# A two-layer decoder trunk on one core: every sum of squares over folded halves, the rotation's sine step as one operation, and a new order

## Chip, core and metric

The kernel runs on one core of one Trainium2 chip. The metric is the device time of one execution in microseconds. The core has five engines with instruction queues of their own: TensorE (PE, matmuls; its weight loads are shown apart as PEld), VectorE (DVE), ScalarE (ACT), GpSimd (POOL) and SyncE (SP, which here only starts transfers). Each works through its queue in order, and they wait for one another through semaphores.

## The reference

Two layers over 512 positions of width 1024, all in float32. What bears on the change:

```python
def rmsnorm(x, g):
    xf = x.astype(jnp.float32)
    y = xf * lax.rsqrt(jnp.mean(xf * xf, axis=-1, keepdims=True) + EPS)
    return y.astype(x.dtype) * g

def rope(x, cos, sin):
    half = x.shape[-1] // 2
    x1, x2 = x[..., :half], x[..., half:]
    ...
    return jnp.concatenate([x1 * cos - x2 * sin, x2 * cos + x1 * sin], axis=-1)

def hybrid_layer(...):
    h = rmsnorm(x, norm_g)
    aq, ak, av, az, bqk, bv, bi, bf, bo, bz, ga, gb = jnp.split(h @ w_in, idx, axis=-1)
    q = rope(rmsnorm(two_map_heads(aq), q_norm_g), cos, sin)   # 8 heads, 2 maps of 64
    k = rope(rmsnorm(two_map_heads(ak), k_norm_g), cos, sin)
    oa = diff_attention(q, k, v, lam)                          # 8 heads of 128
    oa = rmsnorm(oa, attn_norm_g) * (1.0 - lam_init)
    ya = (oa * jax.nn.silu(az)) @ w_out_a
    ...
    hb = mlstm_chunkwise(mq, mk, mv, i_pre, f_pre)             # 8 heads of 128
    hb = rmsnorm(hb, mlstm_norm_g)
    yb = (jax.nn.sigmoid(bo) * hb * jax.nn.silu(bz)) @ w_out_b
    u = jax.nn.sigmoid(ga) * ya + jax.nn.sigmoid(gb) * yb
    return x + u @ w_o
```

## The kernel before, in words

**Products.** Every float32 operand of a matmul is split into a high part in a rounded float32 format and a low part, the rest: a copy on ScalarE (`A.copy(hi, src)`, a CAST in the profile) and a subtraction on VectorE (`split`, line 489). A product is then three matmuls: high by high, high by low, low by high (`mm3`, line 493). Weights come in blocks of 128x1024 (`wr`), and are split into `wh` and `wl`. The normalised input stands transposed as `hh` and `hl`. Projections into 512 tokens by 512 columns or 128 features by 512 tokens accumulate in PSUM tiles of 128x512, of which four (`acc`) are in turn. The last projection, `wo`, is done with seven products instead of eight (`seven`, line 763): P1 to P7 are added up in three PSUM chains, X, Y and Z. P5 and then P3 go into the two banks of Y. Between them ScalarE copies what P5 has left there into an SBUF tile, `p5` (line 779), which P7 needs. What P1 leaves in the two banks of X is copied into `s1` in the same way.

**Attention.** For each of eight heads and four query blocks: scores (`sc`), a mask, a maximum, the exponentials (`p`), the difference of the two maps, transpositions (`ut`) into the split tiles `uh` and `ul`, and then the product with the values (`av`, 12 matmuls and splits of 128 to 512 columns). For the output of a head, 128 features by 512 tokens, the mean of squares over the features is a sum over partitions. It is made by matmuls with a 128x128 matrix of ones (`psum_over`, line 1267), whose result, `msp`, has the sum in every partition. The mLSTM heads end alike (`num` in place of `av`); their denominator `den` is such a sum too.

**Two ways to make the sum.** `ms_front` (line 1271) squares the head's output. Unfolded, the square of 128x512 is split (`msh`, `msl`), and two matmuls with ones add it up. Folded, the two halves of the partitions are squared by two operations of 64x512 (`ms`, `fb`), VectorE adds the one to the other, the sum is split into the two halves of one tile (`fo`: partitions 0 to 63 the high part, 64 to 127 the low one), and one matmul with ones adds both up. `foldA` and `foldM` name the heads that are folded, in attention and in mLSTM; `foldD` the denominators, all of them folded already.

**Rotation.** `qk_done` (line 827) takes a block of 512 columns of q and k. VectorE multiplies it with the cosine table into `rot`, and its halves, exchanged, with the sine table into `sq`: one operation for the first halves of all heads, one for the second. The two are then added.

**The order.** Nothing is issued where the code stands. All operations are recorded first (`Recorder`, line 103): the pieces of the projections follow the list `order`, the heads' steps are hung in between at places given by `a0`, `ap`, `attn`, `m0`, `mp`, `ml` and others. Then `schedule` (line 272) sorts them anew: it gives each operation a due time by its place, its successors and the table `bias`, and takes for each engine in turn the ready operation that is due first, by its own costs and margins (`pemargin`, `smargin`, `late` and others). Each engine's queue is issued in this order. Every number in `TUNE` can so move instructions on all engines.

Of the kernel before, what the change touches and what calls it, by code (L numbers as in the profile page):

```python
# [13 lines left out]
ALU = mybir.AluOpType  # L14
# [4 lines left out]
P = 128  # L19
# [16 lines left out]

TUNE = {
    "order": (
# [4 lines left out]
    ),  # L43
    "qkt": 5,
    "gct": 15,
    "gls": 6,
    "glf": 5,
    "attn": (1, 5, 5, 8, 9, 13, 15, 16, 19, 24),
    "a0": 23,
    "ap": 18,  # L50
    "a4": 7,
    "ml": (1, 9, 11, 12, 13, 28),
    "ahead": 3,
    "lc": 7,
    "slack": 4956.0,
    "margin": 72.0,
    "pemargin": 171.8,
    "wait": 333.1,
    "swpen": 701284048.1,
    "smargin": 51.6,  # L60
    "pwait": 0.8,
    "wdiff": 3673.3,
    "wsp": 4,
    "kact": (0, 2),
    "qsq": (1, 3),
    "foldA": (2, 3, 5),
    "foldM": (0, 1, 2, 3, 4, 7),
    "foldD": (0, 1, 2, 3, 4, 5, 6, 7),
    "warm": 18,
    "start": 'x0 ct ng w0 x1 w1 x2 x3',  # L70
    "prods": 'P1 P5 P3 P6 P2 P7 P4',
    "acl": 12,
    "gateA": 9,
    "gateM": 0,
    "actp": (0, 2, 3),
    "m0": 218,
    "mp": 15,
    "m4": 11,
# [366 lines left out]
def kernel(ctx, tc, x, pos, wp, wg, cst, par, pb, ngb, out):  # L445
# [30 lines left out]
    V, A, T = rec.engine("DVE", nc.vector), rec.engine("ACT", nc.scalar), rec.engine("PE", nc.tensor)  # L476
# [3 lines left out]
    def t2(name, dt=F32):  # L480
        return s2.tile([P, S], dt, tag="s2", name=name)
# [19 lines left out]
    ct = cp.tile([P, C_N], F32, name="ct")  # L501
    posi = cp.tile([P, NT], I32, name="posi")
# [10 lines left out]
    ones = cp.tile([P, P], F32R, name="ones")  # L513
# [21 lines left out]
    cosv = cp.tile([P, NT, 32], F32, name="cosv")  # L535
    sinv = cp.tile([P, NT, 32], F32, name="sinv")
# [86 lines left out]
    x1d = dram.tile([S, D], F32, name="x1d")  # L623


    def layer_events(l):
# [200 lines left out]
        def qk_done(c, tt, acc):  # L827
# [584 lines left out]
        for c in range(4):  # L1412
            ps["qk%d" % c] = tok("qk", c, h_tok, qk_done)
# [227 lines left out]
```

## Time and profile before

| | |
|---|---|
| median of 3 runs | 1334.36 us (1334.33 to 1334.86) |
| profiled execution | 1334.56 us |
| its span | 1332.5 us |
| instructions | 17532 |
| TensorE clock granted | 1.00 |
| transfers | 148.14 MB, mean 111 GB/s |

The profile is one execution. A row of instructions reads: line, engine, operation, output<-inputs by the program's names, partitions by elements, count, and then busy time and mean duration, or (in a tile's view) the least, median and largest duration in ns with the first and the last start in us. A row of the timeline reads: start, duration, engine, line, operation, and in brackets the idle time before it with what ended it. Since all operations are issued by one helper, nearly all have line 441. The names say more: `msp_a` is the sum of squares of an attention head, `msp_b` that of an mLSTM head, `wo_P` the seven products. A matmul's duration reaches into those of its neighbours, so the distance from one start to the next is what it takes of the queue.

### The profile page before, as it was taken

To read this page: it belongs to the slowest core of one execution; us is meant where nothing else is said; L and a number is where in the kernel's file an instruction comes from. 1 tells how busy PE (TensorE), PEld (TensorE's weight loads), DVE (VectorE), ACT (ScalarE), POOL (GpSimd) and SP (SyncE) were. 2 spreads that over 40 slices of the span, in tenths; PEclk is the share of its full clock that TensorE was granted. 3 is DMA by queue.
4 is the path that set the end of the run, shared out by engine and by line. 5 is a ranking of instruction groups with operands and counts; after the bars stand their busy time and mean duration, and the time that the engine had idled before them with its cause. 6 is when DMAs were issued, how large, how long until landed. Compare 5 with 4: busy or idle time off the path is not lost.

```text
span 1332.5 us, 17532 instructions
## 1 busy us (share of the span) xinstructions
PE 1325.0 (99%) x6200; PEld 1095.0 (82%) x6200; DVE 1018.0 (76%) x1846; ACT 907.8 (68%) x1836; POOL 36.9 (3%) x44
## 2 busy tenths in 40 slices
PE   9999999999999999999999999999999999999998
PEld 7888888888888888888788888888888888888886
DVE  7898899786259968755888988997852699687566
ACT  6878798877247858743667787889762489687343
POOL 1000000000000000000200000000000000000000
PEclk9999999999999999999999999999999999999999
DMA  5222222223333443554833122222332344354646
GB/s 188 87 67 78 80 83 64 91 79 99 95 103 112 149 123 113 146 155 128 248 112 95 49 95 64 79 76 83 82 112 79 128 119 141 99 135 135 170 122 182
DMA packets 51272, 148.14 MB, mean 111 GB/s; under 512 B 6096, under 2 KB 12880, under 8 KB 51184
## 3 DMA queue, kind: packets, MB, share of 16 engines
q1 hardware_dynamic: 48880, 138.63, 32.9%
q0 software_dynamic: 2304, 8.39, 3.6%
q8 instruction: 49, 0.80, 0.2%
q14 instruction: 39, 0.32, 0.1%
HBM read 142.74 MB, written 4.26 MB: 110 GB/s over the span
## 4 chain that ended last, share of the span: by engine, by line
PE 98%; ACT 1%; DMA 0%; SPq 0%; DVE 0%; issue 0%; DVEq 0%
PE qk L441 13%; PE av L441 9%; PE az L441 7%; PE bv L441 7%; PE bqk L441 7%; PE bz L441 7%; PE bo L441 7%; PE gb L441 7%; PE ga L441 7%; PE woa L441 7%; PE wob L441 7%; PE wo_P L441 6%; PE sc L441 3%; PE num L441 2%; PE ms L441 1%; PE ut L441 1%
## 5 line engine op out<-in xcount | busy, mean ns | idle before, releaser
L441 ACT CAST wh<-wr 128x1024 fp32r<-128x1024 f32 (+1 forms) x206 | 214.8, 1045 | 190.0 <-PE ga L441 36.3
L441 DVE TENSOR_TENSOR wl<-wr,wh 128x1024 fp32r<-128x1024 f32 (+1 forms) x208 | 248.9, 1200 | 99.7 <-ACT wh L441 98.9
L441 PE MATMUL qk<-wh,hh 128*128 128x512 f32 x256 | 96.1, 401 | 0.5 <-ACT hh L441 0.5
L441 PE MATMUL qk<-wh,hl 128*128 128x512 f32 x256 | 95.3, 400 | 0.1
L441 PE MATMUL qk<-wl,hh 128*128 128x512 f32 x256 | 94.8, 396 | 0.5 <-DVE wl L441 0.5
L441 ACT ACTIVATE p<-sc,mx,rq 128x128 f32<-128x128 f32 (+3 forms) x128 | 78.8, 618 | 16.2 <-DVE mx L441 15.6
L441 PE MATMUL woa<-oa,wh 128*128 128x512 f32 x256 | 87.8, 390 | 0.0
L440 ACT ACT_TABLE_LOAD x65 | 83.4, 1283 | 1.1
L441 PE MATMUL wob<-ob,wh 128*128 128x512 f32 x256 | 83.4, 389 | 0.0
L441 PEld LDWEIGHTS qk<-wl,hh 128*128 128x128 f32 x256 | 48.0, 188 | 10.2 <-DVE wl L441 0.9
L441 PEld LDWEIGHTS wob<-ob,wh 128*128 128x128 f32 x256 | 48.1, 188 | 10.1
L441 PEld LDWEIGHTS qk<-wh,hl 128*128 128x128 f32 x256 | 48.0, 188 | 10.0 <-DVE hl L441 0.4
L441 PEld LDWEIGHTS qk<-wh,hh 128*128 128x128 f32 x256 | 47.7, 188 | 10.0 <-ACT hh L441 0.9
L441 PEld LDWEIGHTS woa<-oa,wh 128*128 128x128 f32 x256 | 47.8, 188 | 9.7
L441 DVE TENSOR_REDUCE mx<-sc 128x2 f32<-128x256 f32 (+1 forms) x64 | 52.5, 821 | 1.1
L441 PE MATMUL bqk<-hh,wl 128*128 128x512 f32 x128 | 50.3, 393 | 0.0
L441 PE MATMUL bo<-hh,wl 128*128 128x512 f32 x128 | 50.2, 392 | 0.0
L441 PE MATMUL bo<-hl,wh 128*128 128x512 f32 x128 | 50.1, 391 | 0.0
L441 PE MATMUL bo<-hh,wh 128*128 128x512 f32 x128 | 50.0, 391 | 0.0
L441 PE MATMUL bqk<-hl,wh 128*128 128x512 f32 x128 | 50.0, 393 | 0.0
L441 PE MATMUL az<-hh,wh 128*128 128x512 f32 x128 | 49.8, 397 | 0.0
L441 PE MATMUL gb<-hl,wh 128*128 128x512 f32 x128 | 49.8, 392 | 0.0
(309 smaller groups left out, 3695.9 us busy)
## 6 DMA issues: line engine op xcount, KB each, us to landing
wr<-in_wp_dram SPq DMA_DIRECT2D x204, 512.0 KB, 3.5
ws_wo<-in_wp_dram POOLq DMA_DIRECT2D x12, 512.0 KB, 6.8
dd<-rows SPq DMA_DIRECT2D x16, 256.0 KB, 4.3
em<-rows SPq DMA_DIRECT2D x16, 256.0 KB, 4.0
dd<-rows SPq DMA_DIRECT2D x16, 192.0 KB, 4.8
x<-in_x_dram SPq DMA_DIRECT2D x4, 512.0 KB, 7.4
dd<-rows SPq DMA_DIRECT2D x16, 128.0 KB, 6.0
ws_wo<-in_wp_dram SPq DMA_DIRECT2D x4, 512.0 KB, 5.2
```

The costliest lines, as they stand in the source:

```text
L440: self.tc.keep_in_program_order(self.nc.scalar.preload_act_table_set(self.SET_NAME[o["load"]]))
L441: self.tc.keep_in_program_order(getattr(o["e"], o["fn"])(*o["a"], **o["k"]))
```

## The change

Three things change. `foldA` and `foldM` name all heads, so the ten attention heads and the four mLSTM heads that were left (0, 1, 4, 6, 7 and 5, 6 of each layer) are folded too. The two sine products of a rotation become one, whose input is read with its halves exchanged by a negative step. The table that sets the order gets other numbers nearly everywhere; of it two lines are shown.

```diff
-    "foldA": (2, 3, 5),
-    "foldM": (0, 1, 2, 3, 4, 7),
+    "foldA": (0, 1, 2, 3, 4, 5, 6, 7),
+    "foldM": (0, 1, 2, 3, 4, 5, 6, 7),
...
-    "pemargin": 171.8,
+    "pemargin": 141.0,
...
-            for hf in range(2):
-                o = 32 * hf
-                V.tensor_tensor(
-                    s4[:, :, :, o : o + 32],
-                    a4[:, :, :, 32 - o : 64 - o],
-                    stab[:, tt, :, o : o + 32].unsqueeze(2).to_broadcast([P, 2, 4, 32]),
-                    ALU.mult,
-                )
+
+            a5, s5_ = (x.rearrange("p (i g h d) -> p i g h d", i=2, g=4, h=2) for x in (acc, r2))
+            stb = stab[:, tt].rearrange("p i (h d) -> p i h d", h=2).unsqueeze(2).to_broadcast([P, 2, 4, 2, 32])
+            V.tensor_tensor(s5_, a5[:, :, :, ::-1, :], stb, ALU.mult)
             V.tensor_tensor(rq, rq, r2, ALU.add)
```

The program has 6200 matmuls before and 6186 after; ScalarE has 66 loads of activation tables in both. Three places show how the order moves.

First, TensorE where P5 ends and P3 begins, in the output projection of layer 1 (`wo1`). `P5_0` and `P5_1` are the two banks, `wh211` and `wl211` the last block of P5's weights, `wh212` the first of P3's. Before:

```order
L441 MATMUL wo1_P5_0_2149<-wl211_2144,uhY1_2_2131 128x512
L441 MATMUL wo1_P5_0_2149<-wh211_2143,ulY1_2_2132 128x512
L441 MATMUL wo1_P5_1_2150<-wh211_2143,ulY1_2_2132 128x512
L441 MATMUL wo1_P5_1_2150<-wh211_2143,uhY1_2_2131 128x512
L441 MATMUL wo1_P5_1_2150<-wl211_2144,uhY1_2_2131 128x512
L441 MATMUL wo1_P5_1_2150<-wh211_2143,ulY1_2_2132 128x512
L441 MATMUL wo1_P5_0_2149<-wh212_2147,uhY1_0_2084 128x512
```

And after:

```order
L441 MATMUL wo1_P5_0_2149<-wh211_2143,uhY1_2_2131 128x512
L441 MATMUL wo1_P5_1_2150<-wh211_2143,uhY1_2_2131 128x512
L441 MATMUL wo1_P5_0_2149<-wl211_2144,uhY1_2_2131 128x512
L441 MATMUL wo1_P5_1_2150<-wl211_2144,uhY1_2_2131 128x512
L441 MATMUL wo1_P5_0_2149<-wh211_2143,ulY1_2_2132 128x512
L441 MATMUL wo1_P5_1_2150<-wh211_2143,ulY1_2_2132 128x512
L441 MATMUL wo1_P5_0_2149<-wh212_2147,uhY1_0_2089 128x512
```

The first bank's last matmul of P5 stood five places ahead of P3's first matmul into that bank, and stands two ahead now. On ScalarE the cast of `wh213` is now issued ahead of the copy of that bank.

Second, ScalarE at the same step of layer 0. Before:

```order
L441 CAST wh102_1115<-wr102_1114 128x1024
L441 COPY s1_wo0_1108<-wo0_P1_0_1104 128x512
L441 COPY p5_wo0_1117<-wo0_P5_0_1112 128x512
L441 COPY p5_wo0_1117<-wo0_P5_1_1113 128x512
L441 CAST wh103_1118<-ws0_wo_0_1033 128x1024
L441 COPY s1_wo0_1108<-wo0_P1_1_1105 128x512
```

And after:

```order
L441 CAST uhB0_2_1092<-ua0_545 128x512 x2
L441 CAST wh102_1115<-wr102_1114 128x1024
L441 COPY s1_wo0_1108<-wo0_P1_0_1104 128x512
L441 COPY s1_wo0_1108<-wo0_P1_1_1105 128x512
L441 COPY p5_wo0_1117<-wo0_P5_0_1112 128x512
L441 COPY p5_wo0_1117<-wo0_P5_1_1113 128x512
```

Both copies of P1's banks now stand ahead of those of P5's. On TensorE the distance from P5's last matmul into its first bank to P3's first is five in both orders here.

Third, the sum of squares of attention head 6 in layer 0, on ScalarE: `ms` and `fb` are the squares of the two halves, `fo` the folded tile, `p` and `uh` belong to head 7, `wh42` is a block of weights. Before, unfolded:

```order
L441 ACTIVATE ms_a0_6_624<-av0_6_623 128x512
L441 ACTIVATE p0_7_0_629<-p0_7_0_629,sums0_7_0_630 128x128
L441 CAST msh_a0_6_625<-ms_a0_6_624 128x512
L441 CAST wh42_632<-wr42_631 128x1024
L441 ACTIVATE p0_7_1_636,sums0_7_1_637<-sc0_7_1_634,mx0_7_1_635,rq0_3_494 128x256
```

And after:

```order
L441 ACTIVATE ms_a0_6_624<-av0_6_623 64x512
L441 ACTIVATE fb_a0_6_625<-av0_6_623 64x512
L441 ACTIVATE p0_7_1_636,sums0_7_1_637<-sc0_7_1_634,mx0_7_1_635,rq0_3_494 128x256
L441 CAST uh0_7_638<-ut0_7_0_640 128x128
L441 ACTIVATE p0_7_1_636,sums0_7_1_637<-sc0_7_1_634,mx0_7_1_635,rq0_3_494 128x256
L441 CAST fo_a0_6_626<-ms_a0_6_624 64x512
L441 CAST wh42_632<-wr42_631 128x1024
```

One more square and two exponentials of head 7 now stand ahead of the cast that the sum waits for. On TensorE 16 matmuls of 512 columns, four of 384 and one transposition stand between the head's last `av` matmul and its `msp` matmul in the new order, which in the old one has two.

More of the change, by code (lines that the diff above doesn't have):

```diff
@@ L38 @@
     "order": (
[4 rows of a table removed]
[4 rows of a table added]
     ),
     "qkt": 5,
-    "gct": 15,
-    "gls": 6,
-    "glf": 5,
+    "gct": 10,
+    "gls": 3,
+    "glf": 7,
     "attn": (1, 5, 5, 8, 9, 13, 15, 16, 19, 24),
@@ L51 @@
     "a4": 7,
-    "ml": (1, 9, 11, 12, 13, 28),
+    "ml": (2, 9, 12, 12, 13, 28),
     "ahead": 3,
-    "lc": 7,
+    "lc": 4,
     "slack": 4956.0,
     "margin": 72.0,
-    "pemargin": 171.8,
+    "pemargin": 141.0,
     "wait": 333.1,
-    "swpen": 701284048.1,
-    "smargin": 51.6,
-    "pwait": 0.8,
+    "swpen": 1431518759.4,
+    "smargin": 17.1,
+    "pwait": 0.6,
     "wdiff": 3673.3,
@@ L71 @@
     "prods": 'P1 P5 P3 P6 P2 P7 P4',
-    "acl": 12,
-    "gateA": 9,
-    "gateM": 0,
+    "acl": 18,
+    "gateA": 7,
+    "gateM": 3,
     "actp": (0, 2, 3),
-    "m0": 218,
+    "m0": 224,
     "mp": 15,
-    "m4": 11,
+    "m4": 24,
     "slots": 20,
-    "bias": {'av': 27450.0, 'msp_a': -4350.0, 'wl': 2400.0, 'wo': -3700.0, 'woh': -4650.0, 'ht': 29150.0, 'taz': -4050.0, 'ga': 16050.0, 'gt': -8800.0, 'p': -300.0, 'wo1_P': 23900.0, 'out_0_dram': -5900.0, 'p5_wo': -4950.0, 'rot': 12650.0, 'dq': -4400.0, 'oa': 450.0, 'dd': 30900.0, 'num': 20100.0, 'ld': -4700.0, 'ws1_wo': -1200.0, 'gw': -1100.0, 'hl': -350.0, 'sc': -1400.0, 'uz': -3750.0, 'mk': 7250.0, 'sbz': 550.0, 'az': 10300.0, 'posi': -650.0, 'msl_d': 1650.0, 's1_wo': 1700.0, 'wob': 50.0, 'msh_d': 6450.0, 'sq': -1600.0, 'warm': 3150.0, 'bo': -400.0, 'sdl': 200.0, 'ml': 15800.0, 'fo_b': 11200.0, 'ws0_wo': -900.0, 'wt1_wo': 1300.0, 'pb': 2000.0, 'sbo': 5350.0, 'qkt': 2000.0, 'junk': 6150.0, 'ulZ': 7650.0, 'bv': 650.0, 'bqk': -1750.0, 'uh': -3950.0, 'ms_b': -1550.0, 'gi': 1000.0, 'ob': 250.0, 'uy': 1750.0, 'gcol': -750.0, 'ms': 11250.0, 'cosv': -4100.0, 'ms_a': 1450.0, 'ones': 2450.0, 'msh_b': 6650.0, 'x1d': -1650.0, 'qt': 1100.0, 'qk0_2x': -6300.0, 'fb_a': 4650.0, 'saz': 900.0, 'xr': -2300.0, 'fb_b': 900.0, 'wo0_P': 450.0, 'qk1_0x': 1950.0, 'fb_d': -5800.0, 'msh_a': 2700.0, 'ulA': -150.0, 'ang': 150.0, 'rnh': 1400.0, 'gft': 6600.0, 'gct': 200.0, 'gc': -300.0, 'mql': -1200.0, 'rows': 150.0, 'kl': -700.0, 'posf': -150.0, 'zw': 2400.0, 'qk1_2x': -3000.0, 'gf': 450.0, 'qk0_0x': -50.0, 'uhY': 7150.0, 'qs': 3050.0, 'qy': 250.0, 'ul': -500.0, 'msl_a': 2800.0, 'uhZ': 7800.0, 'lneps': -950.0, 'gm': -4350.0, 'lq': 450.0, 'x': -3700.0, 'eps': -700.0, 'sgb': 150.0, 'wr': -400.0, 'wt0_wo': -300.0, 'stab': 8000.0, 'xn': 1200.0, 'qss': 150.0, 'den': 2000.0, 'msl_b': 950.0, 'rn': -150.0, 'glf': 900.0, 'ss': 4250.0, 'bz': -100.0, 'sdh': -200.0, 'em': -250.0, 'uhB': 850.0, 'rq': 250.0, 'sinv': -1650.0},
@@ L81 @@
-    "drain": 251.9,
-    "risk": 295.5,
-    "late": 912.7,
+    "bias": {'av': 11300.0, 'msp_a': -4450.0, 'wl': 1150.0, 'wo': -3700.0, 'woh': -4650.0, 'ht': 30450.0, 'gt': -8950.0, 'wo1_P': 19850.0, 'out_0_dram': -8700.0, 'num': 25350.0, 'hl': -600.0, 'sc': -850.0, 'mk': 10050.0, 'msl_d': 1650.0, 'msh_d': 6450.0, 'bo': -1900.0, 'qkt': 5700.0, 'ulZ': 24350.0, 'uh': -2300.0, 'gi': -2950.0, 'ob': -5650.0, 'msh_b': 6650.0, 'msh_a': 2700.0, 'kl': -600.0, 'msl_a': 2800.0, 'msl_b': 950.0, 'ulY': 5350.0, 'bz': -4050.0, 'qk': 400.0, 'gb': -1050.0, 'rows': 4150.0, 'saz': 800.0, 'ms_a': -4000.0, 'dd': -1800.0, 'warm': 4950.0, 'uhZ': -1300.0, 'ks': 16750.0, 'wo0_P': 300.0, 'gw': 650.0, 'az': -300.0, 'wob': -450.0, 'ct': -250.0, 'rot': 1100.0, 'ones': -12550.0, 'lneps': -13350.0, 'ua': 4100.0, 'posf': 6400.0, 'gf': 3450.0, 'xn': 2850.0, 'gcol': -4800.0, 'ga': 50.0, 'sdh': 1100.0, 'qk1_0x': 8400.0, 'uhY': 4150.0, 'x': 700.0, 'qt': 4400.0, 'den': -100.0, 'ld': -1200.0, 'p5_wo': 16250.0, 'wt1_wo': 4700.0, 'sinv': -5050.0, 'sbo': 5250.0, 'em': -8500.0, 'ms_b': 4100.0, 'gft': 3750.0, 'sums': -450.0, 'sgb': 4050.0, 'sdl': -2800.0, 'x1d': 11600.0, 'ws0_wo': 900.0, 'rn': 950.0, 'cv': 12800.0, 'oa': 200.0, 'bqk': 4550.0, 'lq': 250.0, 'ul': 200.0, 'wt0_wo': -2750.0, 'fo_a': 150.0, 'gct': -250.0, 'pb': -2100.0, 'ml': 1600.0, 'uhA': -2300.0, 'uy': -450.0, 'junk': 3150.0, 'wr': 400.0, 'sbz': 600.0, 'mq': -400.0, 'rq': 450.0, 'fb_a': 1300.0, 'mx': 350.0, 'fb_b': -1050.0, 'ut': 1550.0, 'taz': -250.0, 'ng': -1350.0, 'stab': 650.0, 'xr': -1250.0, 'zeroc': -650.0, 'cosv': -400.0, 'glf': 150.0, 'uhB': 1250.0, 'bv': 1000.0, 's1_wo': -2000.0, 'ang': 2850.0, 'mql': -300.0, 'eps': -200.0, 'qk0_0x': 400.0, 'wh': -100.0, 'ws1_wo': -1900.0, 'ss': -1450.0, 'tbz': -2050.0, 'hh': 100.0, 'ulA': 100.0, 'uz': -500.0, 'ms': -300.0, 'posi': 700.0},
@@ L84 @@
+    "drain": 405.0,
+    "risk": 308.5,
+    "late": 751.9,
 }
```

8 rows, old and new, of the table TUNE are left out of this document.

## The prediction

> **What bounds the kernel now.** I read the page's engine table first, then the view of TensorE's waits, the chain that ended last, and a table by stretches.
>
> ```profile
> span 1332.5 us, 17532 instructions
> PE 1325.0 (99%) x6200; PEld 1095.0 (82%) x6200; DVE 1018.0 (76%) x1846; ACT 907.8 (68%) x1836; POOL 36.9 (3%) x44
> PE warm L441 <- DVE ml L441: 1.6, 1, 1.6
> PE qk L441 <- ACT hh L441: 0.5, 1, 0.5
> PE ht L441 <- DVE junk L441: 0.5, 2, 0.3
> PE qk L441 <- DVE wl L441: 0.5, 1, 0.5
> PE wo_P L441 <- ACT p_wo L441: 0.3, 1, 0.3
> PE wo_P L441 <- ACT wh L441: 0.3, 1, 0.3
> 21.95 13.41 PE qk L441 x59
> 468.08 14.74 PE bv L441 x65
> ```
>
> TensorE (PE) is busy for 99% of the span, and the six waits are all that it has: 3.7 us. The first four lie before the first full group of projections; two, in the output projection, come later. The last two rows are unbroken pieces of the chain: 59 matmuls of 512 columns in 13.41 us are 227 ns each from start to start, 65 in 14.74 us also 227 ns. So the kernel is a queue of matmuls: what is taken out of it shortens the end by 227 ns a matmul, and another engine counts only where it makes PE wait.
>
> The page of the Trainium skill "Perfetto Trace Analysis", section "Identifying the Most-Contended Engine", says that a matmul engine's busy share is no measure of its headroom, and to judge by the weight loads. They are at 82% here; by that rule PE would have room left, but the 227 ns repeat in a chain of 65, so there is no slack to gain by order alone.
>
> ```profile
> 12.00:120.00 108.00, 107.80 (x531) 89.02 (x530) 100.27 (x244) 84.29 (x236) 1.90 (x2) 1.00 0.27 85
> 120.00:310.00 190.00, 190.00 (x926) 156.51 (x925) 165.07 (x355) 157.66 (x391) 3.80 (x4) 1.00 0.26 82
> 310.00:640.00 330.00, 330.00 (x1499) 274.78 (x1498) 220.24 (x304) 195.26 (x271) 7.22 (x8) 1.00 0.41 123
> ```
>
> The columns are the length, then the busy time of PE, weight loads, VectorE (DVE), ScalarE (ACT), GpSimd, the granted clock, and DMA. In layer 0's attention VectorE is at 93%, then 87%; ScalarE at 78%, then 83%; in the mLSTM stretch 67% and 59%. Layer 1 repeats this. The clock is 1.00 in all three.
>
> The profiled execution took 1334.56 us, 2.0 us of them around its span; the median of the three runs is 1334.36. I work out a difference against the profiled one and apply it to the median.
>
> **Sums of squares folded.** Ten attention heads (0, 1, 4, 6, 7 of each layer) and four mLSTM heads (5, 6 of each) change form.
>
> ```profile
> L441 PE MATMUL msp_a<-msl_a,ones x10: 389/395/398, 89.3 to 976.5; 128*128 128x512 f32 x10
> L441 PE MATMUL msp_b<-msl_b,ones x4: 389/394/397, 529.7 to 1207.7; 128*128 128x512 f32 x4
> L441 ACT ACTIVATE fb_a<-av x6: 595/596/597, 150.4 to 916.8; 64x512 f32<-64x512 f32 x6
> L441 DVE TENSOR_TENSOR ms_a<-ms_a,fb_a x6: 682/683/684, 151.0 to 917.4; 64x512 f32<-64x512 f32 x6
> L441 DVE TENSOR_TENSOR fo_a<-ms_a,fo_a x6: 685/685/687, 153.1 to 918.8; 64x512 fp32r<-64x512 f32 x6
> L441 DVE TENSOR_TENSOR msl_a<-ms_a,msh_a x10: 672/687/693, 84.0 to 975.5; 128x512 fp32r<-128x512 f32 x10
> ```
>
> Each unfolded head has two matmuls over `ones` (`msh`, `msl`), a folded one has one: 10 + 4 = 14 matmuls leave the queue. Their rows say about 395 ns, but that is a matmul's own duration, which overlaps its neighbours; the queue gets shorter by 227 ns each. 14 x 0.227 = **-3.18 us**. Half the partitions take no less time (685 against 687 ns), so each fold adds one Square (596 ns) on ScalarE and one addition (683 ns) on VectorE: over 14 heads 8.3 and 9.6 us of work. At 76% and 68% they lie beside matmuls. Without that cover, PE would wait about 1.3 us a head for the two operations.
>
> Here the skill speaks against the change: "TensorE: Matmul & The Clock Gate", section "Back-to-back issue gap", gives about 131 ns for a 512-column matmul in a real stream of loads and matmuls. By it the 14 would give back 1.83 us, not 3.18. The trace disagrees, with 227 ns in both chains, so the sum keeps 227.
>
> **The sine step.**
>
> ```profile
> 31.79 0.69 DVE L441 TENSOR_TENSOR rot<-qk,ctab 128x512 f32<-128x512 f32 x1
> 32.39 0.75 DVE L441 TENSOR_TENSOR sq<-qk,stab 128x256 f32<-128x256 f32 x2
> L441 DVE TENSOR_TENSOR sq<-qk,stab x64: 390/418/426, 32.4 to 880.3; 128x256 f32<-128x256 f32 x64
> ```
>
> The 64 products of 256 columns become 32 of 512. The pair takes 0.75 us, the cosine product of 512 columns 0.69: 0.06 us saved, 32 times, 1.9 us of VectorE time. No row shows an operand read with its halves exchanged. The nearest, the cosine product, has the same sources in kind (PSUM and a table), so I take 0.69; the other end is two passes, 2 x 0.69, which would add 32 x 0.63 = 20 us of VectorE time in the attention. PE waits for none of this now, so the term is 0, and at the worse end it raises the risk below.
>
> **The new order: the output projection.** Product P3 of the seven-product form is accumulated onto P5's banks, so its first matmul waits until ScalarE has copied P5 (`p5`). In layer 1 before:
>
> ```profile
> 1299.55 0.62 PE L441 MATMUL wo_P<-wh,ulY 128*128 128x512 f32 x2
> 1300.12 0.60 ACT L441 COPY p_wo<-wo_P 128x512 f32<-128x512 f32 x1
> 1300.46 0.39 PE L441 MATMUL wo_P<-wh,ulY 128*128 128x512 f32 x1
> 1300.77 0.50 PE L441 MATMUL wo_P<-wh,uhY 128*128 128x512 f32 x1
> ```
>
> P5's last matmul into its first bank starts at 1299.55, the copy ends at 1300.72, P3 starts at 1300.77: 1.22 us. Before, P3's first stands five places behind that matmul (5 x 0.227 = 1.14), so PE loses 0.08. In the new order it stands two behind (0.45), and the loss is 1.22 - 0.45 = 0.77: **+0.69 us**. A cast of weights (`wh213`) now stands ahead of the copy on ScalarE, between it and the `s1` copies. The buffer that it writes was freed 16 matmuls earlier, so I take it to be over in time; at the other end it holds the copy up by half of its 1.05 us.
>
> In layer 0 the count stays at five, but the copy was late:
>
> ```profile
> 640.80 0.57 ACT L441 COPY s_wo<-wo_P 128x512 f32<-128x512 f32 x1
> 641.19 0.39 PE L441 MATMUL wo_P<-wh,ulY 128*128 128x512 f32 x1
> 641.28 1.07 ACT L441 COPY p_wo<-wo_P 128x512 f32<-128x512 f32 x2
> 641.91 0.50 PE L441 MATMUL wo_P<-wh,uhY 128*128 128x512 f32 x1 [0.34 <-ACT p_wo L441]
> ```
>
> PE went from 641.19 to 641.91, 0.72 us where 0.23 would do: 0.49 lost, since ScalarE came out of another copy only at 641.28. The new order puts both `s1` copies ahead of it (0.57 each) where one was, and the trace cannot say when ScalarE comes to the cast before them. Bounds: the wait stays (0), or falls to layer 1's 0.08 (-0.41); halfway, **-0.2 us**.
>
> **The new order: how much stands between a head and its sum.** PE executes in order, so a fold that is late stops everything behind its `msp` matmul: projections, scores, transposes. The fold's chain, twice in the trace, and the two operations on weights that may stand inside it (the page's groups, mean ns of one):
>
> ```profile
> 149.26 0.58 ACT L441 ACTIVATE ms_a<-av 64x512 f32<-64x512 f32 x1
> 153.14 0.69 DVE L441 TENSOR_TENSOR fo_a<-ms_a,fo_a 64x512 fp32r<-64x512 f32 x1
> 256.41 0.45 PE L441 MATMUL av<-ul,av 128*128 128x512 f32 x1
> 256.89 0.59 ACT L441 ACTIVATE ms_a<-av 64x512 f32<-64x512 f32 x1 [1.10 <-PE av L441]
> 258.84 0.62 ACT L441 CAST fo_a<-ms_a 64x512 fp32r<-64x512 f32 x1 [0.75 <-DVE ms_a L441]
> 259.49 0.69 DVE L441 TENSOR_TENSOR fo_a<-ms_a,fo_a 64x512 fp32r<-64x512 f32 x1
> 260.93 0.56 ACT L441 ACTIVATE p<-sc,mx,rq 128x256 f32<-128x256 f32 x1
> 261.62 0.58 ACT L441 ACTIVATE p<-sc,mx,rq 128x256 f32<-128x256 f32 x1
> L441 ACT CAST wh<-wr 128x1024 fp32r<-128x1024 f32 (+1 forms) x206 | 214.8, 1045 | 190.0 <-PE ga L441 36.3
> L441 DVE TENSOR_TENSOR wl<-wr,wh 128x1024 fp32r<-128x1024 f32 (+1 forms) x208 | 248.9, 1200 | 99.7 <-ACT wh L441 98.9
> ```
>
> From the first Square to the finished fold it took 153.83 - 149.26 = 4.57 us for head 2 and 260.18 - 256.89 = 3.29 for head 5; the difference is other work on the same engines. In the new order head 6 has the least cover: 16 matmuls of 512 columns, four of 384 and one transposition, by 227 ns and in proportion 16 x 0.227 + 4 x 0.17 + 0.11 = 4.4 us; head 7 has 21 x 0.227 = 4.8, head 5 about 5.0, head 0 about 5.3. The mLSTM heads have 24 or more, over 5.4. Head 6's own chain is head 5's 3.29 plus two exponentials put between, 0.69 apart in the rows above, less the 0.75 that ScalarE stood idle there before its cast: 3.29 + 1.38 - 0.75 = 3.9, and half a microsecond for the way from PE and back. That is the cover, within a tenth. Head 7 has a cast of weights (1.05 us) and its `wl` subtraction (1.20) inside its chain, one after the other: 0.6 + 0.6 + 1.05 + 1.2 + 0.69 = 4.1, with half a microsecond for the way 4.6 against 4.8. I take 0.1 in each layer, **+0.2 us**; bounds 0 and 0.7 (4.57 plus 0.5 against 4.4) in each.
>
> **The sum.** -3.18 + 0.69 - 0.2 + 0.2 = -2.5, and about -0.1 for waits under 0.1 us in the old order that need not come back. -2.6 on 1334.36 gives **1331.8 us**. The bound of 0.2% (about what a measurement tells from no change) is 2.67 us: 1331.69 below, 1337.03 above. The forecast stands just inside it.
>
> **The rivals.**
>
> *The order also removes old waits.* The view of waits leaves 2.1 us behind the first of 1.6; the 0.3 for `wh` and the 1.5 of the first matmuls could shrink if casts and norms come earlier. For: the new table moves rows on all engines. Against: the first 13 us read almost alike in both orders. If half of the 2.1 goes and layer 0's copy is in time: 1331.8 - 1.0 - 0.2 = 1330.6 us.
>
> *The fold is late, and it gets slower.* The mechanism is the wait at `msp` of heads 0, 5, 6 and 7. If a cast and a subtraction of weights (1.05 + 1.20) come on top of head 5's 3.29 in each of them, the chain is 5.5, with the way 6.0, against covers of 5.3, 5.0, 4.4 and 4.8: 4.5 us a layer, 9 in both, 1340.6. It turns slower at 5.2 us over the forecast, 0.65 us at each of the eight. For: VectorE is at 93% early, 20 us more go there if exchanged halves take two passes, and head 7 has one cast and one subtraction inside already. Against: head 6 has its cast behind the fold, and head 2's 4.57 made PE wait nowhere. A quarter of a microsecond at each of the eight, 2 us, gives 1333.8, no change.
>
> *The 14 matmuls are worth less.* At 131 ns each, 1.83 us: 1331.8 + 1.35 = 1333.1. Against: the two chains.
>
> **How the numbers follow.** The sum as it stands 0.56, with a range of its own from 1330.9 to 1332.8 (the copy's and the folds' bounds): a little under half of it lies below 1331.69, so 0.26 faster and 0.30 no change. Old waits go too 0.21, faster. Late folds of a small size 0.09 no change, of the full size 0.10 slower. The 131 ns 0.04, no change. Faster 0.47, same 0.43, slower 0.10. The range reaches to the first rival below (and a quarter of a microsecond further) and to the quarters of a microsecond above: 1330.3 to 1334.0.
>
> **What would show it.** 6186 matmuls on PE; `msp` rows with `fo` alone, x16 each; in the view of waits `wo_P` behind `p_wo` twice, 0.5 to 0.8 us of lost time in layer 1, less than 0.5 in layer 0; the pieces of the chain still at 227 ns; the sine step x32 at about 687 ns; busy time of ScalarE and of VectorE up about 8 us each. A row "msp_a <- DVE fo_a" or idle time before `msp` of heads 6 and 7 would prove the forecast too low; a sine step over a microsecond, or chain pieces under 220 ns a matmul, would prove its prices wrong.

## The result, and the profile after

The changed kernel takes 1336.71 us (median of 20 runs, 1335.19 to 1338.33), the kernel before 1334.31 us in its 20 runs (1334.04 to 1335.81). The ratio is 1.0016, with a 95% interval from 1.0010 to 1.0022: slower by 0.16%, where 0.2% faster had been forecast. So 14 matmuls went, and the kernel became 2.4 us longer. The profiled execution took 1337.23 us, half a microsecond above the median. The head of its page:

```profile
span 1335.5 us, 17544 instructions
PE 1324.2 (99%) x6186; PEld 1092.9 (82%) x6186; DVE 1026.3 (77%) x1828; ACT 914.4 (68%) x1850; POOL 37.0 (3%) x44
```

The counts are as forecast: 6186 matmuls, and 8.3 us more on VectorE. TensorE's busy time fell by 0.8 us, but the span grew by 3.0. What is new stands in the view of TensorE's waits (in total, times, longest):

```profile
PE msp_a L441 <- DVE fo_a L441: 2.1, 2, 1.4
PE ms L441 <- DVE dd L441: 1.9, 2, 1.1
PE wo_P L441 <- ACT p_wo L441: 0.6, 2, 0.4
```

The first two are not in the view of before; each comes once in each layer. To find what they wait for, I go back from each to what its releaser had waited for. First the sum of attention head 7, layer 0, in the timeline:

```profile
304.65 0.43 DVE L441 TENSOR_TENSOR dd<-dd,ct 128x256 f32<-128x256 f32 x1 [1.73 <-DMA dd<-rows]
305.12 0.51 ACT L441 ACTIVATE dd<-dd,gcol 128x256 f32<-128x256 f32 x1 [1.22 <-DVE dd L441]
305.53 0.57 ACT L441 ACTIVATE ms_a<-av 64x512 f32<-64x512 f32 x1
308.94 0.69 DVE L441 TENSOR_TENSOR fo_a<-ms_a,fo_a 64x512 fp32r<-64x512 f32 x1
303.81 0.44 PE L441 MATMUL av<-ul,av 128*128 128x512 f32 x1
308.64 0.39 PE L441 MATMUL woa<-oa,wl 128*128 128x512 f32 x1
309.77 0.47 PE L441 MATMUL msp_a<-fo_a,ones 128*128 128x512 f32 x1 [0.75 <-DVE fo_a L441]
```

`dd` is the decay matrix of mLSTM head 0, whose rows come by DMA from a scratch array. VectorE stands 1.73 us before a mask addition, since the rows are still on their way; ScalarE stands 1.22 us before the exponential of the same piece; and only behind that exponential, in ScalarE's queue, comes the first square of head 7. The head's last `av` matmul starts at 303.81 and is over a little after 304.2, but the square starts at 305.53. From there the fold takes 309.63 - 305.53 = 4.10 us, just what the prediction had worked out. PE goes from 308.64 to 309.77, 1.13 us where 0.23 would do: 0.90 us lost. In layer 1 VectorE stands 2.36 us before the same addition, and PE loses 1.54 us (1.77 from start to start).

The second wait, at mLSTM head 7, in SyncE's queue, on VectorE and on TensorE of layer 0:

```profile
535.41 0.33 SPq L441 DMA_DIRECT2D wr<-in_wp_dram  x1
535.79 1.85 SPq L441 DMA_DIRECT2D dd<-rows  x4
537.68 0.90 SPq L441 DMA_DIRECT2D ws_wo<-in_wp_dram  x2
545.23 0.43 DVE L441 TENSOR_TENSOR dd<-dd,ct 128x256 f32<-128x256 f32 x1 [1.48 <-DMA dd<-rows]
546.71 1.22 DVE L441 SCALAR_TENSOR_TENSOR dd<-ms,dd 128x1024 f32<-128x1024 f32 x1
547.98 0.39 PE L441 MATMUL ms<-mq,mk 128*128 128x256 f32 x1 [1.10 <-DVE dd L441]
```

Again a mask addition waits for rows; behind it in VectorE's queue stand a subtraction of weights and the product `dd<-ms`, which frees the bank that PE's next score matmul needs. PE loses 1.26 us here and 0.96 in layer 1. Together the two places lose 4.7 us.

In the kernel before, VectorE also stood and waited for these rows, but the product came later:

```profile
539.30 0.43 DVE L441 TENSOR_TENSOR dd<-dd,ct 128x256 f32<-128x256 f32 x1 [1.15 <-DMA dd<-rows]
544.18 1.23 DVE L441 SCALAR_TENSOR_TENSOR dd<-ms,dd 128x1024 f32<-128x1024 f32 x1
```

There it starts 4.88 us after the mask addition, with five other operations between the two; now it starts 1.48 us after it, with one between. So a wait for these rows is not new. In layer 0 it is a third of a microsecond longer (1.48 against 1.15 us), in layer 1 as long as before (1.17 against 1.16). What is new is that what PE needs stands close behind it.

The chain that ended last says the same. Among its longest pieces are now four transfers of rows, for the two places in both layers; the chain of before has none:

```profile
297.04 7.52 DMA dd<-rows
537.21 7.93 DMA dd<-rows
956.97 8.15 DMA dd<-rows
1197.83 7.63 DMA dd<-rows
```

The third loss shows in no view of waits. The four transpositions of the gates (`gct`, 8 columns) stood in one run before, and stand in three now. TensorE before, then after:

```profile
129.71 0.39 PE L441 MATMUL av<-wh,hl 128*128 128x512 f32 x1
130.03 0.41 PE L441 MATMUL gct<-ct,gi 8*128 8x8 f32 x4
130.37 0.50 PE L441 MATMUL av<-wh,hh 128*128 128x512 f32 x1
130.71 0.40 PE L441 MATMUL av<-wl,hh 128*128 128x512 f32 x1
```

```profile
94.44 0.39 PE L441 MATMUL qk<-wh,hh 128*128 128x512 f32 x1
94.76 0.23 PE L441 MATMUL gct<-ct,gi 8*128 8x8 f32 x1
94.92 0.50 PE L441 MATMUL qk<-wh,hl 128*128 128x512 f32 x1
95.25 0.40 PE L441 MATMUL qk<-wl,hh 128*128 128x512 f32 x1
95.58 0.22 PE L441 MATMUL gct<-ct,gi 8*128 8x8 f32 x1
95.73 0.50 PE L441 MATMUL qk<-wh,hl 128*128 128x512 f32 x1
96.17 0.28 PE L441 MATMUL gct<-ct,gi 8*128 8x8 f32 x2
96.38 0.50 PE L441 MATMUL qk<-wh,hh 128*128 128x512 f32 x1
96.72 0.39 PE L441 MATMUL qk<-wl,hh 128*128 128x512 f32 x1
```

Before, it is 1.00 us from the first row to the last, with two matmuls of 512 columns in it: 1.00 - 0.45 = 0.55 for the four transpositions. After, 2.28 us with five: 2.28 - 1.14 = 1.14. That is 0.6 us more in each layer, 1.2 in both, for the same transpositions in shorter runs.

With the terms of the prediction as they came out in this execution (the output projection is read further below), the account of the spans is -3.18 for the 14 matmuls, +0.53 and -0.17 in the output projection, +4.7 at the two places and +1.2 for the transpositions: +3.1 us. The span grew by 3.0.

### The profile page after: what moved, and what is told of

Its sections match the earlier page's. It is cut to its first block, busy times and chain, and to the rows that moved or that the text cites. A ratio compares the mean times of both kernels' runs of the same rounds, so it can differ in the third digit from the quotient of the medians.

```text
span 1335.5 us, 17544 instructions
## 1 busy us (share of the span) xinstructions
PE 1324.2 (99%) x6186; PEld 1092.9 (82%) x6186; DVE 1026.3 (77%) x1828; ACT 914.4 (68%) x1850; POOL 37.0 (3%) x44
## 4 chain that ended last, share of the span: by engine, by line
PE 94%; DMA 3%; DVE 1%; ACT 1%; SPq 1%; issue 0%; DVEq 0%
PE qk L441 13%; PE av L441 9%; PE bo L441 7%; PE az L441 7%; PE bqk L441 7%; PE wob L441 7%; PE bv L441 6%; PE woa L441 6%; PE bz L441 6%; PE ga L441 6%; PE gb L441 6%; PE wo_P L441 5%; PE sc L441 3%; DMA dd<-rows 2%; PE num L441 2%; PE ms L441 1%
## 5 line engine op out<-in xcount | busy, mean ns | idle before, releaser
L441 PE MATMUL ga<-hh,wl 128*128 128x512 f32 x128 | 50.4, 394 | 0.0
L441 PE MATMUL ga<-hl,wh 128*128 128x512 f32 x128 | 50.2, 395 | 0.0
L441 PE MATMUL bqk<-hh,wh 128*128 128x512 f32 x128 | 50.1, 391 | 0.0
```

The source lines that it names most:

```text
L441: self.tc.keep_in_program_order(getattr(o["e"], o["fn"])(*o["a"], **o["k"]))
```

## Experiments

Each run is named by its edit, and its time is the median; the ratio is to the kernel before on the same chip. The runs were taken in four sets, in which the kernel before took 1334.68, 1334.51, 1334.82 and 1334.55 us (1334.31 beside the changed kernel). So a difference between two runs of different sets is uncertain by some tenths of a microsecond. Three of the 16 are planned anew; the others keep the order of the changed kernel but for the edit shown or told. Rows are those of layer 0, and layer 1 has the same edit, except in the last section, which is about layer 1 alone.

### The rows of head 0 behind the fold

```diff
 ScalarE: dd_0 128x512, dd_0 128x384
-dd_0 128x256
 ms_a_7, fb_a_7, wh, fo_a_7
+[ua of another block]
+dd_0 128x256
 dd_0 128x128
```

> The changed kernel with two operations moved and nothing else: VectorE's second mask addition of mLSTM head 0's decay matrix dd, and ScalarE's last two exponentials of it, stand behind the fold of attention head 7 instead of inside it, in both layers. Theory A (late rows): in the changed kernel the fold of head 7 starts 1.2 to 1.9 us late because ScalarE stands in its queue before an exponential whose rows are still on their way; the chain itself takes 4.1 us as forecast and fits its cover. Then the two waits of msp_a for fo_a (2.1 us in the view of waits, 2.46 us lost from start to start) go, and the time falls by about 2.4 us, to 1334.3. Rival B (long fold): the fold's five steps with a cast and a subtraction of weights inside are too long by themselves; then msp_a goes on waiting, 0.5 to 1 us in each layer, and the time falls by 0 to 1.2 us. The wait of ms for dd in the mLSTM stays in both.

Measured: 1336.89 us, ratio 1.0016 (1.0007 to 1.0025). By the median nothing was gained. Yet the waits changed (in the fastest of the eleven executions, 1335.90 us, which is the profiled one):

```profile
PE woa L441 <- ACT oa L441: 0.5, 2, 0.4
PE msp_a L441 <- DVE fo_a L441: 0.4, 1, 0.4
```

The wait at `msp_a` is gone in layer 0, and a new one has come at `woa`, a few matmuls on, which needs the head's output `oa`. So theory A fell in this form: the fold did get earlier by 1.2 us, and the rows of head 0 are no longer in the chain that ended last, but the two exponentials had only been moved further down the same tail, ahead of the logarithm and the output. Rival B was not right either, since layer 0's fold fits its cover; in layer 1, where 0.4 us stay, the cast inside the fold waits 0.75 us for its own transfer.

### The rows of mLSTM head 7 ahead of the weights

```diff
 SyncE: em_6
-wr_984
 dd_7 128x512, 128x384, 128x256, 128x128
+wr_984
 ws_wo_979, ws_wo_985
```

> The changed kernel with SyncE's queue changed at one place of each layer: the four transfers of the decay rows of mLSTM head 7 stand ahead of the load of weights that they were queued behind, which waits 6.2 us for its buffer; the rows' own buffer has long been free. All compute engines keep their order. Theory A (late rows): the waits of ms for dd (1.9 us in the view, 2.22 us lost from start to start) are VectorE standing before a mask addition whose rows land 8 us after their issue; with the rows about 6 us earlier they go, and the time falls by 2.2 us, to 1334.5. Rival C (busy VectorE): the product dd<-ms is late because the folds have given VectorE more to do ahead of it; then the wait stays, or falls by less than half, and the time falls by under 1 us. The two waits of msp_a stay in both.

Measured: 1334.11 us, ratio 0.9996 (0.9987 to 1.0005). The wait of `ms` is gone from the view, the rows of head 7 from the chain that ended last, and 2.6 us came back, where 2.2 had been expected. Compute engines had the same order, so rival C falls in its form: their order alone does not make the wait, it takes the late rows as well. Part of the 2.6 is not from this place. The profiled execution lost 1.6 us at attention head 7, where that of the changed kernel lost 2.4, and in layer 0 that head comes before anything that the edit moved; so how late the rows of head 0 land varies from one execution to the next.

### The two loads behind the rows, later

```diff
 SyncE: dd_7 128x512, 128x384, 128x256, 128x128
-ws_wo_979, ws_wo_985
 wr_990
+ws_wo_979, ws_wo_985
 em_7
```

> The changed kernel with the two loads of the output projection's weights (512 KB each), which SyncE starts right behind the rows of mLSTM head 7, moved behind the next load of weights, about 9 us later; compute engines keep their order. Within theory A it tells a late issue from a crowded transfer. If the rows are late because they are started late, their last part still lands some 7 to 8 us after its issue, and the time falls by under 0.7 us, to 1336.0 or above. If they are late because the two loads take their bandwidth, they land in 5 to 6 us, the wait of ms goes, and the time falls by about 2 us, to 1334.7.

Measured: 1334.00 us, ratio 0.9993 (0.9985 to 1.0002), and the wait of `ms` is gone here too. How long the last part of head 7's rows took from issue to landing is the last column of the table of transfers; first the changed kernel, then this run:

```profile
dd<-rows SPq DMA_DIRECT2D x1, 64.0 KB, 7.9
```

```profile
dd<-rows SPq DMA_DIRECT2D x1, 64.0 KB, 6.6
```

The loads cost the rows 1.3 us, and 1.1 in layer 1 (7.6 and 6.5). The mask addition then had its rows just in time. So the run does not decide between late and crowded as was hoped: a late issue and a crowded transfer add up, and taking either away was enough.

The Trainium skill's "DMA: Bandwidth & Descriptors", section "Anatomy of one DMA — SWDGE (gpsimd) path", fits a transfer by 2.0 us and its bytes over 436 GB/s, for another way of issue. Estimated by that, the 64 KB would take 2.2 us, and all four parts, 640 KB in a row, 3.5. The trace has 6.6 with no load behind them, though with one of 512 KB started just ahead.

### Both edits

> Both edits together: mLSTM head 0's mask and exponentials behind the fold of attention head 7, and the rows of mLSTM head 7 ahead of the load of weights. Theory A: both pairs of waits go, 2.46 + 2.22 us, and the time is 1336.7 - 4.7 = 1332.0, within 0.5 us of the forecast of 1331.8; it is then faster than the kernel before by 2.3 us, and its times scatter less than the 3 us of the changed kernel. Rivals B and C: 1334.5 to 1336.5.

Measured: 1334.01 us, ratio 0.9996 (0.9988 to 1.0005): the same as the rows of head 7 alone, and 2 us above theory A. It repeats what the first run said.

### Head 7's tail cleared

On top of the rows of mLSTM head 7 ahead of the weights:

```diff
 ScalarE: dd_0 128x512, dd_0 128x384
-dd_0 128x256
 ms_a_7, fb_a_7
+fo_a_7
 wh_665
-fo_a_7
-dd_0 128x128
 [table load] ua [table load] ms_a_7, ms_a_7, oa_7
+dd_0 128x256, dd_0 128x128
```

> As the run with the rows of mLSTM head 7 ahead of the load of weights, and beside it all foreign work is taken out of attention head 7's tail, in both layers: mLSTM head 0's second mask addition and its last two exponentials stand behind the head's output (oa), the cast of weights behind the fold's cast, the subtraction of weights behind the fold's last subtraction. Theory A2 (crowded tail): the whole tail of head 7, from its last av matmul over the fold and the logarithm to the output that woa waits for, is what counts, and each foreign operation on it costs PE time once the tail is longer than the matmuls beside it. Then both waits, of msp_a for fo_a and of woa for oa, go; the 1.6 us that the run with the rows ahead still lost at head 7 come back, and the time is 1332.5 (1332.0 to 1333.0), two microseconds below the kernel before. Rival (the wait only moves): with the fold earlier, PE waits as long at woa or at the next weights, and the time stays at 1333.6 to 1334.1.

Measured: 1332.74 us, ratio 0.9983 (0.9974 to 0.9993). No wait of `msp_a` is left, and of those at `woa` 0.3 us. 1.4 us came back, on the forecast's side of the rival, and no transfer of rows is left in the chain that ended last.

### Rows out, and weights out

The same in two halves: only the mask addition and the exponentials taken out; or only the cast and the subtraction of weights.

> As the run with the rows of mLSTM head 7 ahead of the load of weights; of the foreign work in attention head 7's tail only mLSTM head 0's mask addition and exponentials are taken out, behind oa, and the cast and the subtraction of weights stay inside the fold. Theory A2 (crowded tail): layer 0's waits go (the fold's chain of 4.1 us fits), in layer 1 half a microsecond stays at msp, since the cast there waits 0.75 us for its own transfer: 1334.1 - 1.0 = 1333.1. Rival (the weights are what counts): 1333.8 to 1334.1.

> The counterpart: only the cast and the subtraction of weights are taken out of the fold of attention head 7, behind it; the mask addition and the exponentials of mLSTM head 0 stay. Theory A2 (crowded tail): the fold is 0.8 us shorter and the waits at msp fall by that much, but cast, exponential and two table loads now stand between the fold and the logarithm, and woa waits for oa instead, 0.5 to 1 us in each layer: the time stays at 1333.7 to 1334.3. Rival (only the fold counts): the waits at msp nearly go and none follow: 1333.0.

Measured: rows out 1332.95 us, ratio 0.9987 (0.9978 to 0.9996); weights out 1336.30 us, ratio 1.0012 (1.0003 to 1.0021). With the rows out nearly all of the 1.4 us is there; the half microsecond expected to stay in layer 1 is not in its view of waits. With the weights out it got slower by 2.2 us, two microseconds above the expected range. The waits of that run, and ScalarE behind the fold:

```profile
PE woa L441 <- ACT oa L441: 2.5, 2, 1.5
```

```profile
308.02 0.62 ACT L441 CAST fo_a<-ms_a 64x512 fp32r<-64x512 f32 x1 [0.75 <-DVE ms_a L441]
308.54 1.05 ACT L441 CAST wh<-wr 128x1024 fp32r<-128x1024 f32 x1
309.91 1.28 ACT L440 ACT_TABLE_LOAD   x1
311.82 1.28 ACT L440 ACT_TABLE_LOAD   x1
316.07 0.62 ACT L441 CAST oa<-ms_a 128x512 fp32r<-128x512 f32 x1 [1.60 <-DVE ms_a L441]
```

ScalarE stands idle for 0.75 us before the fold's cast, while VectorE adds the halves; the cast of weights had stood in that gap for little, and behind the fold it delays the two table loads and the logarithm: the logarithm starts 7.03 us after the first square, against 6.18 in the run that this one is built on. The direction was as theory A2 had it; the waits at `woa` are longer than expected (1.2 and 1.7 us lost from start to start instead of 0.5 to 1), and what the fold gained did not make up for them. With the rows' exponentials out of the tail as well, the same move of the weights cost nothing (1332.74 against 1332.95). So the rows' exponentials were what did not belong there.

### The price of a matmul, and of the sine step

> As the run with the rows of mLSTM head 7 ahead of the load of weights, but each of the 32 msp sums is added up twice by two equal matmuls (the mean then takes half of the sum), right behind each other: 32 matmuls of 512 columns more, no other operation moved. If a matmul is worth 227 ns of the queue, the time rises by 32 x 0.227 = 7.3 us, to 1341.4; by 131 ns each, by 4.2 us, to 1338.3.

Measured: 1340.67 us, ratio 1.0043 (1.0030 to 1.0055). Against the run that it is built on, 6.56 us for 32 matmuls, 205 ns each; between the two profiled spans, 1338.9 and 1331.9, 219 ns. Somewhat under 227, and far from 131. In the two views of waits `msp_a` has 1.3 us without the added matmuls and 0.9 with them; with these 0.4 us the spans give 231 ns, so the shortfall may be no more than a shorter wait.

```diff
-V.tensor_tensor(s5_, a5[:, :, :, ::-1, :], stb, ALU.mult)
+for hf in range(2):
+    V.tensor_tensor(s5_[:, :, :, hf], a5[:, :, :, ::-1, :][:, :, :, hf], stb[:, :, :, hf], ALU.mult)
```

> As the run with the rows of mLSTM head 7 ahead of the load of weights, but the sine step is again two products of 256 columns, one for each half, at the place in VectorE's queue where the single one stands. VectorE is then busy for about 2 us longer (32 x 0.06), beside matmuls; PE waits for none of it. The time stays within 0.3 us of 1334.1. If the sine step was on the path of PE anywhere, the time rises by up to 2 us.

Measured: 1334.14 us, ratio 0.9994 (0.9985 to 1.0003), against 1334.11: no difference. The sine step of the changed kernel, on VectorE:

```profile
L441 DVE TENSOR_TENSOR sq<-qk,stab x32: 669/680/692, 32.4 to 880.4; 128x512 f32<-128x512 f32 x32
```

680 ns, where the cosine product has 682 in the same execution. Exchanged halves cost nothing here.

### The parts of the change alone, planned anew

> The changed kernel with the old table of numbers for the order, but all heads folded and the sine step as one operation: the change without its third part, planned anew by the old numbers. If what the change lost lies in the new order alone (rows late, tail of head 7 crowded, the output projection), the 14 matmuls show: 1334.4 - 3.2 = 1331.2, 1330.8 to 1332.0. If the folds lengthen every head's tail whatever the order, new waits of msp for fo appear here too, and the time is 1333 or above.

> The kernel before with all heads folded, its own table and the two sine products: the first part of the change alone, planned anew. If the folds upset the old plan, it is about as slow as the old table with both operations changed (1351.3, say 1345 or above). If it was the sine step that did, the 14 matmuls show: 1331.2, up to 1333.

> The kernel before with the new table of numbers, but with its old folds (three attention heads, six mLSTM heads) and two sine products: the third part of the change alone, planned anew. The old table with the new operations took 1351.3, 17 us more than either whole version, with waits all over. If table and operations belong together in this way, this one is slower than both as well, by 3 us or more (1338 or above), with waits at other places than the changed kernel. If the new table is good or bad by itself, it stays within 3 us of the changed kernel's waits: 1336.7 + 3.2 = 1339.9 for the 14 matmuls more, or less where the folds had been late: 1335 to 1340.

Measured: all heads folded and one sine step with the old table 1351.29 us, ratio 1.012 (1.0106 to 1.0134); all heads folded and nothing else 1352.58, ratio 1.0123 (1.0106 to 1.0141); the new table with the old operations 1346.07, ratio 1.0079 (1.0065 to 1.0094). The expectation for the old table failed by 20 us; the other two came out slow, as the first theory of each had it. The waits are not those of the changed kernel: with the folds alone (first line), TensorE waits for the output of the last mLSTM head; with the new table alone (second line), for a split in the attention.

```profile
PE wob L441 <- ACT ob L441: 3.2, 2, 1.6
```

```profile
PE av L441 <- DVE ul L441: 2.5, 2, 1.3
```

The parts cannot be added up: +18 us and +11 us apart, +2.4 together. A table of such numbers fits the operations that it was made for, and any change of these plans the whole program anew. So these three say little on the price of a fold. They do show that folds with a plan that doesn't suit them are dear, as the prediction's second rival had it, at other places than it named, and that the new table with the old operations is dear too.

### The gates' transpositions in one run

```diff
-gct, qk, qk, gct, qk, gct x2
+qk, qk, qk, gct x4
```

With the tail cleared:

> As the run with head 7's tail cleared, and the four small transpositions of the gates (gct, 8 columns) of each layer stand in one run again instead of three, as in the kernel before. In the changed kernel the six runs of gct cost 2.2 us more than their matmuls by themselves, in the kernel before two runs 0.6 us. If each change between the projections' matmuls and a transposition costs by the run and not by the transposition, the time falls by 1.4 to 1.6 us, to 1331.2. If it goes by the number of transpositions, which stays at eight, nothing changes: 1332.7.

The rows above give 1.2 us for the difference that this expectation takes as 1.4 to 1.6. In the changed kernel with nothing else:

> The changed kernel with the four gate transpositions of each layer in one run instead of three, and nothing else. Theory (a price by the run): in the changed kernel the short runs of gct lose about 1.2 us more than in the kernel before (0.8 into them and 0.5 out of them, against 0.1 out), and that comes back: 1336.7 - 1.2 = 1335.5, whether other waits are there or not. Rival: the gates wait at another place of the changed kernel, or what is saved here is lost again at head 7, and the time stays within 0.3 us of 1336.7.

Measured: 1331.77 us, ratio 0.9973 (0.9962 to 0.9984), 1.0 us under the tail cleared; and 1335.65 us, ratio 1.0006 (0.9997 to 1.0015), 1.06 us under the changed kernel. In layer 0 the stretch from the matmul ahead of the four transpositions to the second behind them is again 0.99 and 1.00 us with two matmuls of 512 columns in it, as before the change. The price goes by the run: four runs fewer, 0.26 us each by the medians and 0.3 by the rows.

### P5 and P3 apart in layer 1

```diff
 TensorE: P5_0
+P5_0, P5_0, P5_0
 P5_1
-P5_0
 P5_1
-P5_0
 P5_1
-P5_0
 P5_1
 P3_0
```

With the cast of weights moved behind the copies on ScalarE (and its subtraction on VectorE with it), and then with both left where they were:

> As the run with the gates' transpositions together, and in layer 1's output projection P5's last four matmuls into the second bank stand behind its last into the first, so that P3's first stands five places behind that one again; the cast of weights stands behind the two copies on ScalarE. The 0.61 us that PE loses there go down to 0.1, the time falls by 0.5 us, to 1330.7. Rival: the second bank's copy becomes late and the wait moves there; then 1331.2.

> As the run with the gates' transpositions together; in layer 1 P5's last four matmuls into the second bank stand behind its last into the first, but the cast of weights stays ahead of the copy on ScalarE, where the changed kernel has it. The copy can start 0.26 us earlier, when the cast is done: PE still loses 0.35 us before P3, and the time falls by 0.25 us, to 1331.5. If the wait of 1.5 us for wl that came with the moved cast was due to TensorE's order and not to the cast, it comes here too: 1332.6.

Measured: 1332.87 us, ratio 0.9983 (0.9974 to 0.9992), 1.1 us slower than the run that it is built on; and 1331.39 us, ratio 0.9976 (0.9966 to 0.9985). In the first, P3 waits no more, but TensorE stands later for the `wl` of the next block of weights, whose subtraction on VectorE comes behind the moved one (it starts at 1300.85, and at 1299.70 in the run that this one is built on):

```profile
1302.12 0.50 PE L441 MATMUL wo_P<-wl,uhZ 128*128 128x512 f32 x1 [1.34 <-DVE wl L441]
```

The rival had expected another wait than that one. With the cast and the subtraction in place it doesn't come, so moving them was the cause. The last version has the lowest median of all, 3.2 us under the kernel before of its set (1334.55). Whether it gains on the run that it is built on, the times do not show: 1331.77 stood 3.05 us under the kernel before of its own set, with a ratio of 0.9973. In the rows the gain is there: before P3 PE loses 0.27 us (from 1297.24 to 1297.74, where 0.23 would do) instead of 0.61, where 0.35 had been expected.

## Why the prediction was wrong

**What held.** The queue of matmuls, its price within a tenth (205 to 219 ns against 227), the sine step at 0, the length of the fold's chain (4.10 against 4.1), ScalarE's and VectorE's added work (6.6 and 8.3 us, for about 8 each), head 6, whose cover was thought the smallest and which waits nowhere, and the output projection, which the timeline shows in layer 0 and then in layer 1:

```profile
642.39 0.39 PE L441 MATMUL wo_P<-wh,ulY 128*128 128x512 f32 x1
642.94 0.50 PE L441 MATMUL wo_P<-wh,uhY 128*128 128x512 f32 x1 [0.15 <-ACT p_wo L441]
```

```profile
1302.71 0.61 PE L441 MATMUL wo_P<-wh,ulY 128*128 128x512 f32 x2
1303.78 0.50 PE L441 MATMUL wo_P<-wh,uhY 128*128 128x512 f32 x1 [0.45 <-ACT p_wo L441]
```

In layer 0, 0.55 us from start to start where 0.23 would do: 0.32 lost against 0.49 before, -0.17 for a forecast of -0.2, which was the middle between two bounds and came so close by luck. In layer 1 the second of the pair starts at about 1302.94, so 0.84 - 0.23 = 0.61 is lost against 0.08 before, +0.53 for +0.69. The cast ahead of the copy was over in time, 0.24 us before the copy began; it only left no room below that, as the last experiment shows.

**What failed is the step "how much stands between a head and its sum".** It set the fold's chain against the matmuls beside it, and let the chain begin when the last `av` matmul ends. For head 7 the chain did not begin there. The prediction counted the cast and the subtraction of weights inside the fold, but not the three exponentials of another head ahead of the first square, the third of which waits for VectorE, which waits for a transfer. And it looked on no further than `msp`: what PE needs in the end is the head's output, and an operation put behind the fold still stands ahead of that. The term was +0.2. The profiled execution lost 2.4 us there; in the run with the rows of mLSTM head 7 ahead it was 1.6, of which the run with the rows out gave 1.2 back.

**Two terms were not there at all.** The prediction followed SyncE's queue nowhere, and VectorE's only inside the folds. The rows of mLSTM head 7 are queued behind a load of weights that waits for its buffer, with two large loads right behind them now, and the product that TensorE needs now follows closely on the mask addition that waits for them. That is +2.2 us by the rows of the profiled execution, and +2.6 by the run with the rows ahead. And the runs of the gates' transpositions were not counted; they are +1.2 us by the rows, and +1.1 by the run that closes them up.

The account closes to some tenths: 1336.71 - 2.60 - 1.16 - 1.06 = 1331.89, and the forecast was 1331.8. That the two agree to a tenth is luck, since the runs are of different sets. Taken against the kernel before of each set, the same sum is 2.40 - 2.97 - 1.03 - 1.30 = -2.9 us, where -2.6 had been forecast. So the sum was right for what it contained, and the range had no place for what it left out. The rival that ends slower had the right form, a late operation ahead of TensorE, but its price was taken from weights' casts at four heads, and it was a transfer at two places. The rule of 131 ns a matmul is refuted by the 32 added ones. That old waits would go too was not borne out: the 0.3 us for `wh` and most of the first ones are still there.

What stays open: in which shares a late issue and crowded bandwidth made the rows of mLSTM head 7 late, since either cure was enough; whether the old distance between the mask addition and the product on VectorE would have been a third cure, which no run tried; and why a doubled matmul costs 205 to 219 ns and not 227, if it is not the shorter wait.

## What to carry to other kernels

In a kernel that is a full queue of one engine, follow each chain that this engine waits for to its first operation, and read what stands ahead of that in its own queue: an operation that waits for a transfer holds up all behind it, whatever it belongs to. Such a wait can have been there before and have cost nothing, until a new order moves what the bottleneck needs close behind it. When a scheduler has moved everything, compare also the queue that starts transfers (what is each one queued behind, and what is started right behind it) and the number of changes between long matmuls and short transpositions. Work put out of a chain must leave the whole chain, up to the result that the bottleneck needs, or the wait only moves.

## What the runs showed of the hardware

With the folds alone planned by the old table, TensorE waits 1.6 and then 0.7 us at the last mLSTM head, in both layers alike. The stretches around it, layer 0 and then layer 1 (length, busy time of TensorE, weight loads, VectorE, ScalarE, GpSimd, granted clock, DMA):

```profile
573.00:577.50 4.50, 2.23 (x8) 1.01 (x7) 3.54 (x5) 3.97 (x6) 0.91 (x1) 1.00 0.87 330
577.50:582.00 4.50, 4.50 (x21) 3.71 (x20) 2.58 (x4) 1.47 (x3) 0.97 (x2) 1.00 0.96 217
1239.20:1243.40 4.20, 1.93 (x7) 0.71 (x5) 3.27 (x5) 3.67 (x6) 0.78 (x1) 1.00 0.97 359
1243.40:1246.90 3.50, 3.50 (x9) 2.79 (x10) 2.84 (x4) 1.73 (x3) 0.95 (x2) 0.55 0.92 214
```

After the same wait the clock stays at 1.00 in layer 0, and falls to 0.55 for 3.5 us in layer 1, with 9 matmuls where 15 would fit. So the same two waits, 2.3 us in all, were followed in one layer by a further loss of about 1.4 us (six matmuls of 227 ns), and in the other by none. With the old table and both operations changed it is alike: a granted clock of 0.52 from 1244.0 to 1247.5 in layer 1, and 1.00 at the same place of layer 0. The Trainium skill's "TensorE: Matmul & The Clock Gate", section "What's actually happening", has the clock halved after an idle window of about 3.4 us that runs freely; this would let equal waits end differently, and the 3.5 us agree with one window, though TensorE was never idle for that long in one piece.
